# A decoder layer with a retrieved-expert mixer: the fifth densely expanded token tile goes back to gathers

## Chip, cores and metric

The kernel runs on one core of a Trainium2 chip. The metric is the device time of one execution in microseconds (us). Times inside the program come from one profiled execution and count from its first instruction.

## What is computed

One decoder layer over 1024 tokens of width 1024, in float32. A token mixer (gated convolution beside dilated window attention) gives the stream `h`; behind it stands a mixer of retrieved experts (PEER), where the change lies. For each token and each of 8 heads, two sets of 128 keys are scored, the 16 best of each set are paired, and the 16 best pairs are kept: 128 of 16384 experts per token, each with a gate. The expert weights are the rows of two tables, `down` and `up`, of 16384 x 1024 each.

```python
q = (xf @ w_query).reshape(T, PEER_HEADS, 2, PEER_D_HALF)
s = jnp.einsum('thcd,hckd->thck', q, sub_keys)
top_s, top_i = lax.top_k(s, PEER_TOPK)
...
best_s, pos = lax.top_k(cand_s, PEER_TOPK)
idx = jnp.take_along_axis(cand_i, pos, axis=-1)          # T x 8 x 16 expert numbers
gates = jax.nn.softmax(best_s, axis=-1)
...
a = jax.nn.gelu(jnp.einsum('cd,ced->ce', xc, expert_down[ic]))
return jnp.einsum('ce,ced->cd', gc * a, expert_up[ic])    # sum of 128 up rows per token
```

The result is added to the stream, and a last RMS norm scales it.

## The kernel before

The tokens are cut into eight tiles of 128 (128 tokens lie on the 128 partitions). Tiles 0 to 3 are the first half, tiles 4 to 7 the second. The mixer runs for the first half, then for the second; the retrieved experts of the two halves are computed in two different ways, at the same time.

**The side stream (first half, `experts()`).** For each tile and each of 128 experts per token, an indirect DMA on GpSimd's queue gathers one row of `down` per token (128 rows of 4 KB, L851) into one of ROWS = 4 buffers `row`, and VectorE forms its dot product with the token's vector `ut` (L853). After 128 such steps a GELU and the gates give `a`. Then 128 rows of `up` per token are gathered into the same buffers (`rowu`, L867), and VectorE adds each, scaled by its `a`, to `acc` (L869). A norm and a store end the tile. One gather with its VectorE operation is called a step here.

**The dense part (second half, `dense()`).** For all 16384 experts the hidden activations of the 512 tokens are computed by TensorE: `hidden(q)` takes four blocks of 128 experts, loads their `down_t` weights (`raw`, split by L165 and L167 into a high and a low part, so that three matmuls give float32 accuracy), and leaves `ga`. The first STORED = 27 groups go to memory (`a_d`) and are fetched again; four more are held, and the last one is computed late. Meanwhile a routing table is built: `choose` finds experts and gates of a tile, `build` turns them by one-hot matrices (`oa`, `ob`, L940 to L948) and small matmuls (`psg`, L953) into a table of gates per expert and token, which goes to memory as `g_d`. In the up phase, for each of 32 groups, `weigh(q)` multiplies `ga` by the table (`gg`), splits it (`hh`, `hl`), and TensorE multiplies it with the split up rows (`uh`, `ul`, L181 and L182) into PSUM tiles: `held` stays over all groups, `psu` is added to `rest` in SBUF after each (L1067). At the end the sums meet the stream in `h1b` (L1071), and each tile is normed and stored.

**The fifth tile.** `XT = (1,)` makes tile 1 of the first half a mixture: its `down` rows are gathered as above, but after the GELU its gated activations go to `given`, which builds a routing table of them; in the up phase `weigh` reads it as `gx`, splits it (`xh`, `xl`, L978 and L979) and TensorE multiplies it with the same up rows as a fifth tile. So the side stream has 512 down steps and 384 up steps, and the up phase five tiles.

**What sets the order.** The main program yields shares of its work, divided by PACE_B, PACE_C or PACE_D, and the side stream advances by as many steps as have come due. A scheduler then fixes one list per engine. Each engine works its own list through from top to bottom.

Of the kernel before, what the change touches and what calls it, by code (L numbers as in the profile page):

```python
# [8 lines left out]
F32 = mybir.dt.float32  # L9
F32R = mybir.dt.float32r  # L10
I32 = mybir.dt.int32
U32 = mybir.dt.uint32
AF = mybir.ActivationFunctionType
ALU = mybir.AluOpType
# [3 lines left out]
P = 128  # L18
T = 1024
TH = 512  # L20
# [10 lines left out]
ROWS = 4  # L31
TC = 32
NB = 4
PACE_B = 2.0
PACE_D = 2.0
PACE_C = 2.2
RATE_G = 0.8
STORED = 27
HOLD = 4
RAWS = 4  # L40
HILO = 2
# [4 lines left out]
AT_P = 6  # L46
CHOOSE = (0, 1, 2, 3)
ORDER = (0, 1, 2, 3)
TILES = (4, 5, 6, 7, 1)
STB = 2  # L50
XT = (1,)
GXB = 2
XHB = 1
UPS = 7
NW = 2
NS = 2
# [9 lines left out]
def hybrid_layer(ctx, tc, x, xT, pos, rotc, norm_mix, w_proj, w_v, conv_w, w_conv_out, w_attn_out,  # L66
                 gate_bias, w_out, norm_ffn, w_query, sub_keys, down, down_t, up, final_norm, out):
    nc = tc.nc
    V, S, G, PE = nc.vector, nc.scalar, nc.gpsimd, nc.tensor
# [6 lines left out]
    ex = ctx.enter_context(tc.tile_pool(name="ex", bufs=1))  # L76
# [73 lines left out]
    y_d = dram.tile([2, KD, P, TH], F32, name="y_d")  # L150
    s_d = dram.tile([3, P, 16, P], F32, name="s_d")
    a_d = dram.tile([STORED, P, NB, TH], F32, name="a_d")
    g_d = dram.tile([(TH + len(XT) * P) // TC, P, P, TC], F32, name="g_d")


    def row_scale(src):
# [677 lines left out]
            queue.dma_start(out[r, c], acc[:, c])  # L834


    xready = {}

    def experts():
        for tt in ORDER:  # L840
            r = slice(tt * P, tt * P + P)
            if tt:
                for _ in later[tt]:
                    pass
            idx, gate = picked[tt]
            ut = ex.tile([P, D], F32, tag="ut", name="ut")
            SIDE.dma_start(ut, u2_d[r])
            a = ex.tile([P, P], F32, tag="a", name="a")
            for e in range(P):
                row = gt.tile([P, D], F32, tag="row", name="row")  # L850
                G.indirect_dma_start(out=row, out_offset=None, in_=down,  # L851
                                     in_offset=bass.IndirectOffsetOnAxis(ap=idx[:, e:e + 1], axis=0))
                V.tensor_tensor_reduce(out=row, in0=row, in1=ut, scale=1.0, scalar=0.0, op0=ALU.mult,  # L853
                                       op1=ALU.add, accum_out=a[:, e:e + 1])
                yield 1.0
            S.activation(a, a, AF.Gelu)
            if tt in XT:
                ax = ex.tile([P, P], F32, tag=f"ax{tt}", name="ax")
                V.tensor_tensor(ax, a, gate, op=ALU.mult)
                xready[tt] = (idx, ax)  # L860
                continue
            V.tensor_tensor(a, a, gate, op=ALU.mult)
            acc = ex.tile([P, D], F32, tag="acc", name="acc")
            SIDE.dma_start(acc, h1_d[r])  # L864
            for e in range(P):
                row = gt.tile([P, D], F32, tag="row", name="rowu")
                G.indirect_dma_start(out=row, out_offset=None, in_=up,  # L867
                                     in_offset=bass.IndirectOffsetOnAxis(ap=idx[:, e:e + 1], axis=0))
                V.scalar_tensor_tensor(acc, row, a[:, e:e + 1], acc, op0=ALU.mult, op1=ALU.add)  # L869
                yield 1.0  # L870
            st = ex.tile([P, 3], F32, tag="st", name="st")
            nfin = gt.tile([P, D], F32, tag="row", name="nfin")
            SIDE.dma_start(nfin, final_norm.to_broadcast([P, D]))
            S.activation(ut, acc, AF.Square, accum_out=st[:, 0:1])
            finish(acc, r, st, nfin, SIDE)


    def dense():
# [2 lines left out]
        bld = ExitStack()  # L881
        den = bld.enter_context(tc.tile_pool(name="den", bufs=2))
        NG = P // NB
        NT = 4 + len(XT)
        gas = {}

        def hidden(q):
# [18 lines left out]
            yield from choose(lambda hc: s_t[tt][:, hc], True, got)  # L906
            yield from build(got[0], tt * P // TC)

        def given(k):
            while XT[k] not in xready:  # L910
                next(result["side"])
            idx, ax = xready[XT[k]]
            part = den.tile([P, 2, P], U32, tag="part", bufs=1, name="part")
            V.tensor_scalar(part[:, 0], idx.bitcast(U32), 7, None, op0=ALU.logical_shift_right)
            V.tensor_scalar(part[:, 1], idx.bitcast(U32), 127, None, op0=ALU.bitwise_and)
            name = den.tile([P, 2, P], F32, tag="name", bufs=1, name="name")
            V.tensor_copy(name, part)
            yield from build((name[:, 0], name[:, 1], ax), (TH + k * P) // TC)

        def routes():  # L920
            for k in range(len(XT)):
                yield from given(k)
            for tt in range(4):
                yield from chosen(tt)

        def build(srcs, c0):
                sT = den.tile([P, 3, P], F32, tag="sT", bufs=STB, name="sT")
                for j, src in enumerate(srcs):
                    ps = psc.tile([P, P], F32, tag="sc", name="ps_t")
                    PE.transpose(ps, src, ident)  # L930
                    S.copy(sT[:, j], ps)
                for c in range(c0, c0 + P // TC):
                    stg = [den.tile([P, 32, TC], F32, tag="stg", bufs=STG, name="stg") for _ in range(4)]
                    for t4 in range(TC // 4):
                        ps = psc.tile([P, 4, P], F32, tag="sc", name="psg")
                        k0 = (c * TC + t4 * 4) % P
                        i1, i2, gv = (sT[:, j, k0:k0 + 4] for j in range(3))
                        oa = den.tile([P, 4, P], F32, tag="oa", bufs=OBUF, name="oa")
                        ob = den.tile([P, 4, P], F32, tag="ob", bufs=OBUF, name="ob")
                        V.tensor_tensor(oa, iota[:, None, :].to_broadcast([P, 4, P]),  # L940
                                        i1[:, :, None].to_broadcast([P, 4, P]), op=ALU.is_equal)
                        if t4 % 2 == 0:
                            for t in range(4):
                                S.activation(ob[:, t], iota, AF.Abs, bias=i2[:, t:t + 1], scale=-1.0)
                            S.activation(ob, ob, AF.Relu, bias=ones[:, 0:1], scale=-1.0)
                            V.tensor_tensor(ob, ob, gv[:, :, None].to_broadcast([P, 4, P]), op=ALU.mult)
                        else:
                            V.tensor_tensor(ob, iota[:, None, :].to_broadcast([P, 4, P]),  # L948
                                            i2[:, :, None].to_broadcast([P, 4, P]), op=ALU.is_equal)
                            for t in range(4):  # L950
                                S.mul(ob[:, t], ob[:, t], gv[:, t:t + 1])
                        for t in range(4):
                            PE.matmul(ps[:, t], ob[:, t], oa[:, t], start=True, stop=True)  # L953
                        for w in range(4):
                            S.copy(stg[w][:, :, t4 * 4:t4 * 4 + 4],
                                   ps[:, :, 32 * w:32 * w + 32].rearrange("p t i -> p i t"))
                        yield 1.1
                    for w in range(4):
                        nc.sync.dma_start(g_d[c, :, 32 * w:32 * w + 32], stg[w])

        def weigh(q):
            gg = m8.tile([P, TH // TC, NB, TC], F32, tag="big", name="gg")
            nc.sync.dma_start(gg, g_d[:TH // TC, :, NB * q:NB * q + NB].rearrange("c j i t -> j c i t"))
            ga = gas.pop(q)
            hh, hl = bigr("hh"), bigr("hl")
            for ii in range(NB):
                v = ga[:, ii].rearrange("p (c t) -> p c t", t=TC)
                V.tensor_tensor(v, v, gg[:, :, ii], op=ALU.mult)
                split(hh[:, ii], hl[:, ii], ga[:, ii])
            parts = [(hh[:, :, tt * P:tt * P + P], hl[:, :, tt * P:tt * P + P]) for tt in range(4)]  # L970
            for k in range(len(XT)):
                gx = up_p.tile([P, P // TC, NB, TC], F32, tag="gx", bufs=GXB, name="gx")
                c0 = (TH + k * P) // TC
                nc.sync.dma_start(gx, g_d[c0:c0 + P // TC, :, NB * q:NB * q + NB].rearrange("c j i t -> j c i t"))
                xh = up_p.tile([P, NB, P], F32R, tag="xh", bufs=XHB, name="xh")
                xl = up_p.tile([P, NB, P], F32R, tag="xl", bufs=XHB, name="xl")
                view = [t.rearrange("p i (c t) -> p c i t", t=TC) for t in (xh, xl)]
                S.copy(view[0], gx)  # L978
                V.tensor_tensor(view[1], gx, view[0].bitcast(F32), op=ALU.subtract)  # L979
                parts.append((xh, xl))  # L980
            return parts

        ready = {}
# [96 lines left out]
    begin()  # L1080
    for _ in mixer(0):
        pass
    side = result["side"] = experts()
    due = 0.0

    def main():
# [67 lines left out]
```

## Time and profile before

| | us |
|---|---|
| median of 3 runs | 3464.77 |
| lowest and highest run | 3463.74, 3466.05 |
| the profiled execution | 3463.79 |
| its span, first to last instruction | 3462.0 |

| engine | busy, us | share of the span |
|---|---|---|
| TensorE (PE) | 3316.7 | 96% |
| VectorE (DVE) | 2766.8 | 80% |
| ScalarE (ACT) | 1486.4 | 43% |
| GpSimd (POOL) | 1193.4 | 34% |

Read the shares with care: they are means over stages that have different limits. PE's busy time counts matmuls, PEld the weight loads beside them. POOL is busy while it writes a DMA's descriptors, not while the data move.

### The profile page before, as it was taken

What the parts mean: (1) busy time and instruction counts of PE and PEld (TensorE: products, weight loads), DVE (VectorE), ACT (ScalarE), POOL (GpSimd) and SP (SyncE); (2) the same over time, 40 slices, a digit from 0 to 9 for tenths busy, and PEclk for the clock granted to TensorE, in tenths of its full rate; (3) what the DMA queues carried; (4) which work ended last, traced back from release to release, by engine and by line L of the source; (5) the groups of instructions that cost most, each with busy time, mean ns of one, the idle gap of its engine ahead of it and who ended that gap; (6) DMA issues with size and microseconds to landing.
All of it is one profiled execution on the core that took longest, in us unless ns stands there. A gap on an engine that the chain in (4) does not pass through costs nothing.

```text
span 3462.0 us, 47124 instructions
## 1 busy us (share of the span) xinstructions
PE 3316.7 (96%) x15923; PEld 2702.5 (78%) x15923; DVE 2766.8 (80%) x5646; ACT 1486.4 (43%) x3371; POOL 1193.4 (34%) x944
## 2 busy tenths in 40 slices
PE   7999999999979999989899999999999999999998
PEld 6787877888767877667777878888887788887787
DVE  4333345689998888988999999998887888888887
ACT  3444445443333445333325776887632222222222
POOL 0000000004554235555444334354444334444443
PEclk9999999999979999999999999999999999999999
DMA  4232335669987678898898989989898999989996
GB/s 129 78 110 89 122 107 180 246 210 323 308 281 256 227 246 298 305 340 309 301 329 300 342 288 343 349 313 366 334 323 311 331 326 332 337 324 329 332 348 230
DMA packets 364307, 948.08 MB, mean 274 GB/s; under 512 B 33952, under 2 KB 127648, under 8 KB 356640
## 3 DMA queue, kind: packets, MB, share of 16 engines
q1 hardware_dynamic: 232016, 465.27, 38.8%
q0 software_dynamic: 132048, 479.78, 38.4%
q8 instruction: 126, 2.06, 0.2%
q14 instruction: 117, 0.96, 0.1%
HBM read 843.15 MB, written 95.49 MB: 271 GB/s over the span
## 4 chain that ended last, share of the span: by engine, by line
PE 28%; issue 16%; DVE 14%; DMA 14%; POOL 8%; ACT 2%; POOLq 0%; DVEq 0%; SPq 0%; ACTq 0%
DMA rowu<-in_up,idx 6%; PE ps L178 6%; PE ps L176 6%; PE ps L177 6%; POOL row L851 4%; DVE row L853 4%; DMA row<-in_down,idx 4%; POOL rowu L867 3%; PE psg L953 2%; DVE lo L167 2%; DVE acc L869 1%; DMA g_d<-stg 1%; DMA gg<-g_d 1%; PE held L177 1%; PE held L178 1%
## 5 line engine op out<-in xcount | busy, mean ns | idle before, releaser
L851 POOL DMA_INDIRECT row<-in_down,idx x512 | 641.5, 1253 | 896.6 <-DVE a L853 504.3
L867 POOL DMA_INDIRECT rowu<-in_up,idx x384 | 528.4, 1376 | 622.5 <-DVE acc L869 496.6
L165 ACT CAST hi<-raw 128x1024 fp32r<-128x1024 f32 x368 | 388.0, 1054 | 713.5 <-PE ps L177 506.8
L853 DVE CUSTOM_DVE_ANT_0 row<-row,ut 128x1024 f32<-128x1024 f32 x512 | 618.8, 1214 | 62.8 <-DMA row<-in_down,idx 60.8
L167 DVE TENSOR_TENSOR lo<-raw,hi 128x1024 fp32r<-128x1024 f32 x368 | 448.4, 1219 | 264.6 <-ACT hi L165 252.6
L178 PE MATMUL ps<-vhi,lo 128*128 128x512 f32 (+1 forms) x1408 | 536.7, 382 | 22.0 <-DVE lo L167 21.7
L869 DVE SCALAR_TENSOR_TENSOR acc<-rowu,a,acc 128x1024 f32<-128x1024 f32 x384 | 491.2, 1279 | 66.4 <-DMA rowu<-in_up,idx 64.3
L176 PE MATMUL ps<-vhi,hi 128*128 128x512 f32 (+1 forms) x1408 | 531.8, 378 | 12.3 <-ACT hi L165 7.6
L177 PE MATMUL ps<-vlo,hi 128*128 128x512 f32 (+1 forms) x1408 | 530.6, 377 | 0.0
L176 PE MATMUL ps<-uhi,hi 128*128 128x512 f32 x1024 | 408.3, 400 | 6.1 <-ACT hi L165 3.6
L178 PE MATMUL ps<-uhi,lo 128*128 128x512 f32 x1024 | 408.5, 399 | 2.5 <-DVE lo L167 2.3
L177 PE MATMUL ps<-ulo,hi 128*128 128x512 f32 x1024 | 408.3, 399 | 0.5 <-DVE ulo L182 0.5
L178 PEld LDWEIGHTS ps<-vhi,lo 128*128 128x128 f32 x1408 | 269.7, 192 | 75.7 <-DVE lo L167 31.9
L176 PEld LDWEIGHTS ps<-vhi,hi 128*128 128x128 f32 x1408 | 270.4, 192 | 61.3 <-ACT hi L165 12.4
L177 PEld LDWEIGHTS ps<-vlo,hi 128*128 128x128 f32 x1408 | 269.7, 192 | 45.0
L177 PE MATMUL held<-ul,hh 128*128 128x512 f32 x624 | 246.5, 395 | 10.0 <-DVE ul L182 10.0
L178 PE MATMUL held<-uh,hl 128*128 128x512 f32 x624 | 244.1, 391 | 0.0
L176 PEld LDWEIGHTS ps<-uhi,hi 128*128 128x128 f32 x1024 | 193.8, 189 | 52.7 <-ACT hi L165 5.5
L178 PEld LDWEIGHTS ps<-uhi,lo 128*128 128x128 f32 x1024 | 193.6, 189 | 47.4 <-DVE lo L167 5.8
L176 PE MATMUL held<-uh,hh 128*128 128x512 f32 x624 | 230.5, 393 | 0.0
L177 PEld LDWEIGHTS ps<-ulo,hi 128*128 128x128 f32 x1024 | 193.6, 189 | 42.8 <-DVE ulo L182 1.7
L864 POOL DMA_DIRECT2D acc<-h_d x3 | 1.8, 615 | 640.9 <-DMA h_d<-h 640.9
(350 smaller groups left out, 6133.8 us busy)
## 6 DMA issues: line engine op xcount, KB each, us to landing
raw<-in_w_proj SPq DMA_DIRECT2D x128, 512.0 KB
raw<-in_down_t SPq DMA_DIRECT2D x128, 512.0 KB
rawu<-in_up SPq DMA_DIRECT2D x128, 512.0 KB
g_d<-stg SPq DMA_DIRECT2D x80, 512.0 KB
gg<-g_d SPq DMA_DIRECT2D x32, 1024.0 KB
a_d<-ga SPq DMA_DIRECT2D x27, 1024.0 KB
ga<-a_d SPq DMA_DIRECT2D x27, 1024.0 KB
raw<-in_w_query SPq DMA_DIRECT2D x48, 512.0 KB
```

The costliest lines, as they stand in the source:

```text
L165: S.copy(hi, raw)
L167: V.tensor_tensor(lo, raw, hi.bitcast(F32), op=ALU.subtract)
L176: PE.matmul(ps, l[0], r[0], start=first, stop=False)
L177: PE.matmul(ps, l[0], r[1], start=False, stop=False)
L178: PE.matmul(ps, l[1], r[0], start=False, stop=last)
L851: G.indirect_dma_start(out=row, out_offset=None, in_=down, in_offset=bass.IndirectOffsetOnAxis(ap=idx[:, e:e + 1], axis=0))
L853: V.tensor_tensor_reduce(out=row, in0=row, in1=ut, scale=1.0, scalar=0.0, op0=ALU.mult, op1=ALU.add, accum_out=a[:, e:e + 1])
L864: SIDE.dma_start(acc, h1_d[r])
L867: G.indirect_dma_start(out=row, out_offset=None, in_=up, in_offset=bass.IndirectOffsetOnAxis(ap=idx[:, e:e + 1], axis=0))
L869: V.scalar_tensor_tensor(acc, row, a[:, e:e + 1], acc, op0=ALU.mult, op1=ALU.add)
L953: PE.matmul(ps[:, t], ob[:, t], oa[:, t], start=True, stop=True)
```

## The change

Tile 1 is no longer in the dense part: `XT` and all that hangs on it is removed (`given`, the fifth part of `weigh`, the larger `g_d`), so its up rows are gathered and summed as for tiles 0, 2 and 3. With it come other paces and a smaller STORED.

```diff
-PACE_B = 2.0
-PACE_D = 2.0
-PACE_C = 2.2
+PACE_B = 1.8
+PACE_D = 1.8
+PACE_C = 2.0
-STORED = 27
+STORED = 24
-TILES = (4, 5, 6, 7, 1)
+TILES = (4, 5, 6, 7)
-XT = (1,)
-GXB = 2
-XHB = 1
...
             S.activation(a, a, AF.Gelu)
-            if tt in XT:
-                ax = ex.tile([P, P], F32, tag=f"ax{tt}", name="ax")
-                V.tensor_tensor(ax, a, gate, op=ALU.mult)
-                xready[tt] = (idx, ax)
-                continue
             V.tensor_tensor(a, a, gate, op=ALU.mult)
...
-        NT = 4 + len(XT)
+        NT = 4
...
-        def given(k):
-            while XT[k] not in xready:
-                next(result["side"])
...
-            yield from build((name[:, 0], name[:, 1], ax), (TH + k * P) // TC)
...
         def routes():
-            for k in range(len(XT)):
-                yield from given(k)
             for tt in range(4):
                 yield from chosen(tt)
...
-            for k in range(len(XT)):
-                gx = up_p.tile([P, P // TC, NB, TC], F32, tag="gx", bufs=GXB, name="gx")
...
-                S.copy(view[0], gx)
-                V.tensor_tensor(view[1], gx, view[0].bitcast(F32), op=ALU.subtract)
-                parts.append((xh, xl))
             return parts
```

Lines move up by 3 to 33 with it: in the new kernel the down gather is L846, its dot product L848, the up gather L857 and its sum L859, the addition of `held` to `h1b` L1038.

The list of POOL, where tile 1 passes from down rows to what follows. Before:

```order
L864 DMA acc<-h_d 128x1024
L851 DMA row<-in_down,idx 128x1024 x125
L847 DMA ut<-u_d 128x1024
L851 DMA row<-in_down,idx 128x1024 x125
L867 DMA rowu<-in_up,idx 128x1024 x128
```

The same place in the new list:

```order
L854 DMA acc<-h_d 128x1024
L846 DMA row<-in_down,idx 128x1024 x122
L857 DMA rowu<-in_up,idx 128x1024 x128
L863 DMA nfin<-in_final_norm 128x1024
L846 DMA row<-in_down,idx 128x1024 x3
L842 DMA ut<-u_d 128x1024
L831 DMA out<-acc 128x1024
```

Before, the down rows of tile 1 are followed at once by those of tile 2; now 128 gathers of up rows stand between them, with the norm and the store of the tile.

The list of VectorE, near its end, where the side stream's last sums and the first additions of `held` into `h1b` meet. Before:

```order
L869 SCALAR_TENSOR_TENSOR acc<-rowu,a,acc 128x1024 x2
L979 TENSOR_TENSOR xl<-gx,xh 128x4x4x32
L869 SCALAR_TENSOR_TENSOR acc<-rowu,a,acc 128x1024 x3
L1071 TENSOR_TENSOR h1b_28941<-h1b_28941,held_22681 128x512
L1071 TENSOR_TENSOR h1b_28941<-h1b_28941,psu 128x512
L200 TENSOR_SCALAR st<-st 128x1
L1071 TENSOR_TENSOR h1b_28942<-h1b_28942,psu 128x512
```

The last addition of `held` in the new list (ISA with `row` is a down dot product, ISA `a` the reading of its sum):

```order
L1042 TENSOR_TENSOR sts<-sts 128x1
L848 ISA row,a<-row,ut 128x1024
L848 ISA a 128x1
L1042 TENSOR_TENSOR sts<-sts 128x1
L1038 TENSOR_TENSOR h1b_27664<-h1b_27664,held_21632 128x512
L199 RECIPROCAL sts<-sts 128x1
L848 ISA row,a<-row,ut 128x1024
```

And the end of VectorE's new list:

```order
L848 ISA row,a<-row,ut 128x1024
L848 ISA a 128x1
L852 TENSOR_TENSOR a<-a,ge 128x128
L859 SCALAR_TENSOR_TENSOR acc<-rowu,a,acc 128x1024 x128
L197 TENSOR_SCALAR st<-st 128x1
L199 RECIPROCAL st<-st 128x1
L200 TENSOR_TENSOR st<-st 128x1
L201 TENSOR_TENSOR st<-st 128x1
L202 TENSOR_SCALAR st<-st 128x1
L203 TENSOR_TENSOR st<-st 128x1
L830 SCALAR_TENSOR_TENSOR acc<-acc,st,nfin 128x1024
```

Before, all 896 steps stand ahead of the first addition of `held`. In the new list 796 of 1024 stand ahead of the last one, and 100 dot products and 128 up sums behind it. Counted in the same way, 314 steps stand ahead of the 240th operation of L167 before and 312 now (L164 there), and 598 ahead of the first split of up rows (`ul`) before and 538 now.

## Rows read from the trace of the kernel before

**Rows 1.** The page: busy us (share of the span) and instructions; DMA in all.

```profile
PE 3316.7 (96%) x15923; PEld 2702.5 (78%) x15923; DVE 2766.8 (80%) x5646; ACT 1486.4 (43%) x3371; POOL 1193.4 (34%) x944
...
DMA packets 364307, 948.08 MB, mean 274 GB/s; under 512 B 33952, under 2 KB 127648, under 8 KB 356640
```

**Rows 2.** The stage cuts: VectorE by time, and the instructions of tile `ul`.

```profile
1639.93 1.22 DVE L167 TENSOR_TENSOR lo<-raw,hi 128x1024 fp32r<-128x1024 f32 x1
...
L182 DVE TENSOR_TENSOR ul<-rawu,uh x126: 1209/1216/1239, 2514.2 to 3421.6; 128x1024 fp32r<-128x1024 f32 x126
```

**Rows 3.** Busy time by stage: stretch, its length, then the engines.

```profile
core 0: us, PE busy (x) PEld busy (x) DVE busy (x) ACT busy (x) POOL busy (x), PEclk, DMA share, GB/s
0.00:1640.00 1640.00, 1554.28 (x7659) 1248.02 (x7660) 1164.91 (x2791) 689.41 (x1384) 427.10 (x358) 0.98 0.64 219
1640.00:2514.00 874.00, 839.77 (x4272) 703.69 (x4271) 817.73 (x1816) 556.95 (x1650) 370.71 (x286) 0.99 0.89 327
2514.00:3452.60 938.60, 922.59 (x3995) 750.75 (x3993) 778.08 (x1024) 239.12 (x334) 395.60 (x301) 1.00 0.90 322
...
2514.00:3400.00 886.00, 869.99 (x3767) 707.92 (x3766) 734.63 (x951) 224.87 (x303) 378.97 (x288) 1.00 0.92 330
```

**Rows 4.** The end, by time: start us, us, engine, line, operation, [idle before].

```profile
3426.12 1.86 POOL L867 DMA_INDIRECT rowu<-in_up,idx  x1 [0.65 <-DVE acc L869]
...
3431.34 1.28 DVE L869 SCALAR_TENSOR_TENSOR acc<-rowu,a,acc 128x1024 f32<-128x1024 f32 x1 [1.05 <-DMA rowu<-in_up,idx]
...
3438.52 0.57 POOL L834 DMA_DIRECT2D out<-acc  x1 [9.96 <-DVE acc L833]
...
3452.23 0.39 PE L178 MATMUL held<-uh_end,xl 128*128 128x512 f32 x1
```

**Rows 5.** Groups by line: count, busy us, mean ns, then idle before.

```profile
L867 POOL DMA_INDIRECT rowu<-in_up,idx x384 | 528.4, 1376 | 622.5 <-DVE acc L869 496.6 <-DMA rowu<-in_up,idx 32.0 <-issue 18.8
L869 DVE SCALAR_TENSOR_TENSOR acc<-rowu,a,acc 128x1024 f32<-128x1024 f32 x384 | 491.2, 1279 | 66.4 <-DMA rowu<-in_up,idx 64.3
L167 DVE TENSOR_TENSOR lo<-raw,hi 128x1024 fp32r<-128x1024 f32 x368 | 448.4, 1219 | 264.6 <-ACT hi L165 252.6 <-DMA qp<-rraw 4.9 <-DMA raw<-in_w_proj 4.8
L940 DVE TENSOR_TENSOR oa<-iota,sT 128x512 f32<-128x512 f32 x160 | 105.6, 681 | 7.1 <-PE psg L953 6.2 <-ACT sT L931 0.6 <-issue 0.2
L1067 DVE TENSOR_TENSOR rest<-rest,psu 128x512 f32<-128x512 f32 x120 | 80.2, 679 | 2.3 <-PE psu L178 2.3
L948 DVE TENSOR_TENSOR ob<-iota,sT 128x512 f32<-128x512 f32 x80 | 54.1, 680 | 0.0
L979 DVE TENSOR_TENSOR xl<-gx,xh 128x512 fp32r<-128x512 f32 x32 | 21.8, 680 | 0.0
```

**Rows 6.** One stretch, tile `ps` (weight matmuls), then `psg` (table): PE first.

```profile
2200.00:2500.00 300.00, 241.89 (x1016) 186.98 (x1015) 25.89 (x42) 1.00 0.91 338
...
2200.00:2500.00 300.00, 74.53 (x608) 74.09 (x608) 60.12 (x304) 1.00 0.91 338
```

**Rows 7.** DMA queues from 2514 to 3452.6 us: packets, MB, share.

```profile
q1 hardware_dynamic: 121569, 141.85, 45.5%
q0 software_dynamic: 43776, 159.40, 44.0%
```

**Rows 8.** A sum on VectorE, and the gather that it releases on POOL.

```profile
3381.41 1.28 DVE L869 SCALAR_TENSOR_TENSOR acc<-rowu,a,acc 128x1024 f32<-128x1024 f32 x1 [0.44 <-DMA rowu<-in_up,idx]
...
3382.97 0.94 POOL L867 DMA_INDIRECT rowu<-in_up,idx  x1 [1.39 <-DVE acc L869]
```

**Rows 9.** The densest gathers, POOL by time: first and last of 28.

```profile
943.83 0.94 POOL L851 DMA_INDIRECT row<-in_down,idx  x1 [1.13 <-DVE a L853]
...
998.69 1.58 POOL L851 DMA_INDIRECT row<-in_down,idx  x1 [0.94 <-DVE a L853]
```

**Rows 10.** Instructions of tile `rowu`: ns min/median/max, first and last start.

```profile
L869 DVE SCALAR_TENSOR_TENSOR acc<-rowu,a,acc x384: 1233/1278/1344, 1119.2 to 3431.3; 128x1024 f32<-128x1024 f32 x192
```

More of the change, by code (lines that the diff above doesn't have):

```diff
@@ L152, in hybrid_layer @@
     a_d = dram.tile([STORED, P, NB, TH], F32, name="a_d")
-    g_d = dram.tile([(TH + len(XT) * P) // TC, P, P, TC], F32, name="g_d")
+    g_d = dram.tile([TH // TC, P, P, TC], F32, name="g_d")
     def row_scale(src):
@@ L834, in finish @@
             queue.dma_start(out[r, c], acc[:, c])
-    xready = {}
     def experts():
@@ L907, in chosen @@
             yield from build(got[0], tt * P // TC)
-        def given(k):
-            while XT[k] not in xready:
-                next(result["side"])
[L912 to L917, printed above, removed]
-            yield from build((name[:, 0], name[:, 1], ax), (TH + k * P) // TC)
         def routes():
-            for k in range(len(XT)):
-                yield from given(k)
             for tt in range(4):
@@ L970, in weigh @@
             parts = [(hh[:, :, tt * P:tt * P + P], hl[:, :, tt * P:tt * P + P]) for tt in range(4)]
-            for k in range(len(XT)):
-                gx = up_p.tile([P, P // TC, NB, TC], F32, tag="gx", bufs=GXB, name="gx")
[L973 to L977, printed above, removed]
-                S.copy(view[0], gx)
-                V.tensor_tensor(view[1], gx, view[0].bitcast(F32), op=ALU.subtract)
-                parts.append((xh, xl))
             return parts
@@ L1082, in hybrid_layer @@
         pass
-    side = result["side"] = experts()
+    side = experts()
     due = 0.0
```

## The prediction

> **What bounds the kernel now.** I began with the busy table of the page [rows 1]: TensorE is busy 96% of the span, VectorE 80%, and the DMA engines move 948 MB. A share of the span hides stages with different limits, so I cut the span at two places that can be found in both programs. The first is the 240th weight split of L167, at about 1640 us, when the hidden activations of the dense half begin; the second is the first split of up rows, at 2514 us [rows 2]. The busy times of the stages [rows 3] show TensorE with 840 of 874 us in the middle stage and 923 of 939 us in the last; VectorE has 818 of 874 us in the middle one, so there the two are nearly level, and in the last one VectorE has 17% to spare. Between 2514 and 3400 us a matmul record takes 886/3767 = 0.235 us of wall time. So before the change every matmul taken out of the last two stages is worth close to its time, as long as the program ends with TensorE. It does: the last gather sum starts at 3431.3 us, the last matmul ends at 3452.6 us, and the span ends at 3462.0 us [rows 4]. The stream of gathers is finished 20 us before the dense work; that is the fact to watch.
>
> **What goes.** The fifth tile costs 32 x 2 x 4 x 3 = 768 matmuls of 512 columns in the last stage. Its routing table costs 128 matmuls of the program, 256 records in the trace, in the middle stage, and on VectorE 64 operations of 0.68 us (32 `oa`, 32 `ob`), then 32 splits `xl` of 0.68 us and 60 of the 120 additions into `rest`, also 0.68 us [rows 5]. On the queues go 16 of the 80 writes `g_d<-stg` and the 32 reads `gx<-g_d` of 256 KB.
>
> **What comes.** 128 gathers of 0.5 MB on POOL, and 128 sums of 1.28 us on VectorE [rows 5]; without the dense tile 1024 gather steps have to be done instead of 896. STORED falls from 27 to 24, which moves 12 weight matrices (288 matmuls, 12 splits of 1.22 us) from the middle stage to the last and drops three 1 MB writes and reads.
>
> **What moves, which decides.** VectorE runs its list in order. In the list of before 314 gather steps stand ahead of the first cut, 598 ahead of the second, and all 896 ahead of the first addition of `held`. In the new list it is 312, 538, and at the last addition of `held` (which needs TensorE's last matmul) 796. Behind that addition stand 100 down dot products and 128 up sums, with no dense work left. The paces were lowered from 2.0 and 2.2 to 1.8 and 2.0, which asks for more steps per unit of dense work, but the list itself says that they don't fit: 228 steps come after the dense work. The new kernel has two ends, one behind the other.
>
> **Stage by stage, on the profiled execution's own time.**
> First stage: the lists differ by two gather steps, I leave it at 1640 us.
> Middle stage, 874 us. TensorE loses 288 matmuls at 241.89/1016 = 0.238 us and 256 table records at 74.53/608 = 0.123 us [rows 6], 68.6 + 31.4 = 100 us: 774 us if its idle time stays. VectorE loses 58 steps at 1.28 us, 64 operations of 0.68 us and 12 splits of 1.22 us: 74 + 44 + 15 = 132 us, so 818 - 132 = 686 us; at the share of before, 818/874 = 0.936, that is 733 us. VectorE was the tighter one in the first half of this stage, TensorE in the second; I take 750 us, nearer to VectorE's, and keep 733 to 774.
> Last stage up to the last matmul, 938.6 us. Matmul records go from 3995 to 3995 - 768 + 288 = 3515; at 0.235 us that is 826 us, and at TensorE's busy time alone (922.59/3995 = 0.231) 812 us. The cover is the DMA: its share is 0.90 of 938.6 us, 845 us [rows 3]. 40 fewer gathers are 21 MB at the software queue's price (44.0% of 938.6 us for 159.4 MB, 2.59 us per MB), 54 us; `gx` and three `ga` reads are 11.5 MB at the hardware queue's (45.5% for 141.85 MB, 3.01 us per MB), 35 us; 6.3 MB of weights come to 19 us [rows 7]. 845 - 70 = 775 us; at the share of 0.92 that the stretch 2514 to 3400 us holds [rows 3], 842 us. I take 830 us and keep 812 to 842. VectorE needs 778 - 51 - 22 - 41 + 15 = 679 us there, which fits.
> So the last addition of `held` comes at 1640 + 750 + 830 = 3220 us, 232 us earlier than now. That is the gain.
>
> **The tail.** Before the change no stretch has gathers alone, so I bound a step from both sides. Four row buffers are in use, so four steps share one loop: gather, landing, VectorE's operation, and back to the gather. The last gather starts at 3426.12 us and its sum, which waited for it, at 3431.34 us: 5.22 us, with 1.86 us on POOL [rows 4]. From the end of a sum to the start of the next gather I read 3382.97 - (3381.41 + 1.28) = 0.28 us [rows 8]. The loop is 5.22 + 1.28 + 0.28 = 6.78 us, a step 1.70 us. With the 0.94 us that POOL takes when VectorE stands still [rows 8], the loop is 5.86 us and a step 1.46 us. From the other side: the densest stretch of gathers, from 943.83 to 998.69 us, has 27 steps of 2.03 us [rows 9], with VectorE doing other work between them. I take 1.75 us, because it is a little above the blocked loop, and gathers so close also queue behind each other; ends 1.46 and 2.03. The tail is 228 x 1.75 = 399 us (333 to 463). Behind the last sum the chain stays as now: the sum started at 3431.34 us, the store of `acc` was issued from 3438.52 to 3439.09 us [rows 4], and I add 2 us for its landing: 10 us, 11 with the end of the program.
> Sum: 3220 + 399 + 11 = 3630 us of span, and 1.8 us around it (3463.79 against 3462.0) make 3632 us. The profiled execution lies 1 us below the median of the runs, which I leave aside.
>
> **Why POOL's time in the loop varies.** A gather that started at 3426.12 us while a sum was running took 1.86 us, others 0.94 us [rows 4, 8]; that is the difference between my 1.70 and 1.46. The Trainium skill (SBUF — State Buffer, section "SBUF: two separate sides") says that VectorE and GpSimd share a port pair as an exclusive lock, so that a POOL-issued DMA cannot write its descriptors while VectorE holds it; the trace agrees with 1.86 against 0.94 us.
>
> **Rivals.**
> One: in the tail POOL and VectorE exclude each other at every step. A step is then 1.28 + 0.94 = 2.22 us and the tail 506 us: 1640 + 750 + 830 + 506 + 11 + 2 = 3739 us. For it: 1.86 us is 0.94 and most of a sum. Against it: none of 384 sums took over 1.344 us [rows 10], so VectorE does not wait for POOL. The lock of that page of the Trainium skill, taken strictly, is this case.
> Two: with the dense transfers gone, landings get so short that the tail runs at VectorE's pace, 1.28 us: 292 us, 3525 us in all. Against it: even the unblocked loop gives 1.46 us with four buffers.
> Three, not slower: everything that I count as waiting is queueing behind gathered rows and dense transfers, and goes with them. TensorE then has its busy time alone, 1554 + 740 + 812 = 3106 us [rows 3], and the tail VectorE's: 3106 + 292 + 11 + 2 = 3411 us, faster by 1.5%. It decides from 168 us on beyond my sum, or a step under 1.02 us if the dense work keeps my time; no operation of a step is so short. For it: TensorE is idle 145 us in all. Against it: the first stage, where most of that lies, is unchanged.
> That the change does not do what it says can be excluded by the lists: POOL has 512 up gathers and SP no `gx`.
>
> **How the numbers follow.** The forecast, 3632 us, has 0.78, rival one 0.08, rival two 0.11, rival three 0.03. The ends of the terms add up to 1640 + 733 + 812 + 333 + 13 = 3531 and 1640 + 774 + 842 + 463 + 13 = 3732 us; terms rarely lie at the same end together, so the forecast's own spread is 3545 to 3710 us. For 8 in 10 I reach down to rival two and a little up: 3520 to 3715 us; outside are rivals one and three and some of the forecast. A change of 0.2% is about what a measurement of this kernel can tell from none. Faster by more has rival three alone, 0.03; no change gets 0.01, for the space between rivals two and three; slower 0.96.
>
> **What would show it.** After the change TensorE must be idle for some 400 us at the end, with POOL's L846 and L857 and VectorE's L848 and L859 alone at work; the last matmul should end near 3220 us, and the gather steps behind it number 228. In the tail VectorE waits for DMA at nearly every step and POOL for VectorE. The middle stage should take about 750 us, the last about 830 us. I am wrong if the last matmul comes after 3290 us (then the dense stages were bound by DMA or VectorE after all), if a tail step is under 1.4 or over 2.1 us, or if TensorE works to the end.

## The result and the profile after

The changed kernel takes 3696.03 us (median of 4 runs, 3689.86 to 3699.20), the kernel before 3465.41 us: a ratio of 1.0652, 95% interval 1.0628 to 1.0677. The forecast was 3632 us. The profiled execution took 3689.86 us, with a span of 3688.0 us.

The page's busy table and its 40 slices show it at once. TensorE loses 1027 matmul records and 209 us against [rows 1], and is idle in the last five slices; there the granted clock stands at 0.5, the lower of its two levels (1.2 GHz), and TensorE has no more work.

```profile
PE 3108.1 (84%) x14896; PEld 2531.4 (69%) x14896; DVE 2838.6 (77%) x5609; ACT 1407.7 (38%) x3062; POOL 1401.9 (38%) x1075
...
PE   7999999999899999898999999999899999900000
...
PEclk9999999999799999899999999999999999955555
DMA  4233345778886788988887899998889999888886
```

The same cuts as in [rows 3], and a fourth stretch from the last matmul on (busy us of each engine, granted clock, DMA share, GB/s):

```profile
0.00:1637.50 1637.50, 1558.12 (x7659) 1248.41 (x7660) 1162.04 (x2787) 690.21 (x1384) 409.64 (x356) 0.98 0.65 219
1637.50:2401.20 763.70, 734.78 (x3711) 618.45 (x3710) 699.41 (x1584) 471.35 (x1352) 351.69 (x231) 0.99 0.86 312
2401.20:3230.60 829.40, 815.16 (x3530) 664.50 (x3528) 675.20 (x862) 239.13 (x310) 359.85 (x260) 0.99 0.92 329
3230.60:3688.00 457.40, 0.00 (x0) 0.00 (x0) 301.98 (x381) 6.99 (x16) 280.74 (x230) 0.50 0.80 270
```

The dense work ends 222 us earlier than before (3230.6 against 3452.6 us), and behind it come 457 us in which nothing is full: VectorE is busy 302 us, POOL 281 us, the DMA engines 0.80. That is the picture of a loop that waits for itself: gather, landing, VectorE's operation, and back to the gather into the same buffer. The two places where the engines pass to the tail are the last matmul, and the last addition of `held`, behind which 228 steps follow:

```profile
3230.17 0.39 PE L175 MATMUL held<-uh_end,hl 128*128 128x512 f32 x1
...
3235.92 0.68 DVE L1038 TENSOR_TENSOR h1b<-h1b,held 128x512 f32<-128x512 f32 x1
```

Inside the tail's up part, the instructions of tile `rowu` (ns min/median/max, first and last start) give the step: 220.6 us over 116 intervals, 1.90 us. Over all 228 steps, from the addition at 3235.9 us to the end of the last sum at 3672.3 us, it is 1.91 us.

```profile
L859 DVE SCALAR_TENSOR_TENSOR acc<-rowu,a,acc x117: 1283/1285/1350, 3439.3 to 3659.9; 128x1024 f32<-128x1024 f32 x117
L857 POOL DMA_INDIRECT rowu<-in_up,idx x116: 932/938/1997, 3440.0 to 3658.4; - x116
```

By time, gathers on POOL and sums on VectorE (start us, us, what they waited for):

```profile
3544.81 0.94 POOL L857 DMA_INDIRECT rowu<-in_up,idx  x1 [0.59 <-DVE acc L859]
3547.53 1.89 POOL L857 DMA_INDIRECT rowu<-in_up,idx  x1 [1.79 <-DVE acc L859]
3549.72 1.90 POOL L857 DMA_INDIRECT rowu<-in_up,idx  x1 [0.30 <-DMA rowu<-in_up,idx]
3551.93 1.02 POOL L857 DMA_INDIRECT rowu<-in_up,idx  x1 [0.30 <-issue]
3553.25 1.70 POOL L857 DMA_INDIRECT rowu<-in_up,idx  x1 [0.30 <-issue]
...
3545.98 2.63 DVE L859 SCALAR_TENSOR_TENSOR acc<-rowu,a,acc 128x1024 f32<-128x1024 f32 x2 [1.44 <-DMA rowu<-in_up,idx]
3549.53 2.60 DVE L859 SCALAR_TENSOR_TENSOR acc<-rowu,a,acc 128x1024 f32<-128x1024 f32 x2 [0.92 <-DMA rowu<-in_up,idx]
3552.86 1.28 DVE L859 SCALAR_TENSOR_TENSOR acc<-rowu,a,acc 128x1024 f32<-128x1024 f32 x1 [0.73 <-DMA rowu<-in_up,idx]
3555.85 1.28 DVE L859 SCALAR_TENSOR_TENSOR acc<-rowu,a,acc 128x1024 f32<-128x1024 f32 x1 [1.71 <-DMA rowu<-in_up,idx]
```

The gather of 3544.81 us serves the second sum of the pair at 3549.53 us, which starts near 3550.85 us, 6.0 us later; that sum ends at 3552.13 us and frees its buffer, but the next gather into it starts only at 3553.25 us, 1.1 us later, because POOL was still at the gather of 3551.93 us. In these rows VectorE waits for a landing before every sum or pair of sums. Over 116 such steps, from the records of the trace: 5.64 us from a gather's start to its sum's start (about 5.2 until its last row is written, about 0.4 behind that), 1.29 us for the sum, 0.66 us to the next gather; 7.6 us for four buffers.

The end, two sums in one row and the store behind them:

```profile
3669.72 2.61 DVE L859 SCALAR_TENSOR_TENSOR acc<-rowu,a,acc 128x1024 f32<-128x1024 f32 x2 [0.57 <-DMA rowu<-in_up,idx]
...
3677.60 0.56 POOL L831 DMA_DIRECT2D out<-acc  x1 [9.08 <-DVE acc L830]
```

### The profile page after: what moved, and what is told of

Its sections match the earlier page's. It is cut to its first block, busy times and chain, and to the rows that moved or that the text cites. A ratio compares the mean times of both kernels' runs of the same rounds, so it can differ in the third digit from the quotient of the medians.

```text
span 3688.0 us, 44975 instructions
## 1 busy us (share of the span) xinstructions
PE 3108.1 (84%) x14896; PEld 2531.4 (69%) x14896; DVE 2838.6 (77%) x5609; ACT 1407.7 (38%) x3062; POOL 1401.9 (38%) x1075
## 4 chain that ended last, share of the span: by engine, by line
PE 35%; issue 13%; DVE 12%; DMA 12%; POOL 9%; ACT 2%; POOLq 0%; SPq 0%; DVEq 0%; ACTq 0%
POOL row L846 6%; PE ps L175 5%; PE ps L173 5%; PE ps L174 5%; DMA rowu<-in_up,idx 5%; DMA row<-in_down,idx 4%; DVE row L848 3%; POOL rowu L857 3%; PE held L175 3%; PE held L174 3%; PE held L173 3%; DVE lo L164 2%; PE psg L930 2%; DVE acc L859 1%; PE psu L175 1%
## 5 line engine op out<-in xcount | busy, mean ns | idle before, releaser
L857 POOL DMA_INDIRECT rowu<-in_up,idx x512 | 740.2, 1446 | 818.1 <-DVE acc L859 606.5
L846 POOL DMA_INDIRECT row<-in_down,idx x512 | 636.4, 1243 | 729.3 <-DVE a L848 394.9
L859 DVE SCALAR_TENSOR_TENSOR acc<-rowu,a,acc 128x1024 f32<-128x1024 f32 x512 | 655.4, 1280 | 112.3 <-DMA rowu<-in_up,idx 109.5
L848 DVE CUSTOM_DVE_ANT_0 row<-row,ut 128x1024 f32<-128x1024 f32 x512 | 619.8, 1217 | 138.9 <-DMA row<-in_down,idx 135.6
L164 DVE TENSOR_TENSOR lo<-raw,hi 128x1024 fp32r<-128x1024 f32 x368 | 448.6, 1220 | 271.7 <-ACT hi L162 267.3
L174 PE MATMUL held<-ul,hh 128*128 128x512 f32 x752 | 295.0, 392 | 2.0 <-DVE ul L179 2.0
L175 PE MATMUL held<-uh,hl 128*128 128x512 f32 x752 | 296.1, 394 | 0.0
L173 PE MATMUL held<-uh,hh 128*128 128x512 f32 x752 | 292.6, 390 | 0.0
L178 ACT CAST uh<-rawu 128x1024 fp32r<-128x1024 f32 x126 | 132.2, 1050 | 374.7 <-PE held L175 123.7
```

The costliest lines, as they stand in the source:

```text
L164: V.tensor_tensor(lo, raw, hi.bitcast(F32), op=ALU.subtract)
L173: PE.matmul(ps, l[0], r[0], start=first, stop=False)
L174: PE.matmul(ps, l[0], r[1], start=False, stop=False)
L175: PE.matmul(ps, l[1], r[0], start=False, stop=last)
L178: S.copy(hi, src)
L846: G.indirect_dma_start(out=row, out_offset=None, in_=down, in_offset=bass.IndirectOffsetOnAxis(ap=idx[:, e:e + 1], axis=0))
```

## The experiments

Theory: the change frees TensorE, but the list leaves 228 steps behind the dense work, and each costs a quarter of that loop. Rivals: the steps were badly placed and the dense stages have room for them; the paces or STORED made the kernel slow; something other than the loop sets the step. Ratios are to the kernel before, run on the same chip.

**All steps forced ahead of the end of the dense work.**

```diff
-                    split(uh, ul, raw)
+                    S.copy(uh, raw)
+                    with tc.issue_after(steps[-1].ins):
+                        V.tensor_tensor(ul, raw, uh.bitcast(F32), op=ALU.subtract)
```

Here `steps` holds the VectorE operation of every step that the program has yielded so far.

> The changed kernel, but the split of up rows (ul, L179) is ordered behind the gather steps that the program yielded ahead of it, so that all 1024 steps stand ahead of the last addition of held and none behind it (228 behind it in the changed kernel). Theory: the gathered rows are too many bytes for the dense stages; the DMA queues are busy 657 us of the middle stage and 763 us of the last one in the changed kernel, 228 gathers at 1.39 us add 317 us, and at a share of 0.89 to 0.92 both stages together take 1890 to 1950 us: about 3580 us (3550 to 3615), faster than the changed kernel, still slower than before. Rival 1: the dense stages have room for the steps and only the list was bad: about 3260 us. Rival 2: a step costs its 1.91 us wherever it stands: about 3690 us.

Measured: 3816.8 us, ratio 1.0985 (1.0956 to 1.1014), slower than the changed kernel and than theory and both rivals said. The tail is gone, but the two dense stages took 1016 and 1155 us instead of 764 and 829 us. The middle stage, cut in three, and the up phase:

```profile
1634.90:2400.00 765.10, 736.55 (x3713) 618.72 (x3712) 699.01 (x1586) 470.61 (x1353) 359.39 (x231) 0.99 0.87 312
2400.00:2500.00 100.00, 17.54 (x77) 13.94 (x75) 68.37 (x111) 8.45 (x14) 60.43 (x49) 0.61 0.85 286
2500.00:2651.30 151.30, 2.08 (x4) 1.16 (x4) 99.86 (x136) 3.14 (x4) 94.08 (x80) 0.50 0.84 278
2651.30:3806.00 1154.70, 889.36 (x3448) 698.32 (x3448) 803.96 (x977) 228.34 (x305) 489.62 (x361) 0.87 0.80 280
```

Up to 2400 us the middle stage runs as in the changed kernel. Then TensorE all but stops for 251 us, and the other 128 of the stage's 354 steps go through with hardly any dense work beside them, at 1.9 to 2.1 us each: the forced order did not spread them, it put a second tail into the middle of the program. The first split of up rows now stands behind 666 steps instead of 538, and in ScalarE's list the GELU of a tile (`a`), which needs all dot products of the tile, comes before the next copies to `uh` (us in total, times, longest us):

```profile
ACT a L853 <- DVE a L850: 172.7, 1, 172.7
PE held L173 <- ACT uh L1016: 186.6, 1, 186.6
PE held L174 <- DVE ul L1018: 46.4, 1, 46.4
```

In the up phase TensorE waits for VectorE's `ul`, which stands behind gather steps in the list:

```profile
PE held L174 <- DVE ul L1018: 216.0, 44, 46.4
PE held L173 <- ACT uh L1016: 70.5, 16, 13.6
```

The DMA share is 0.80 there, so the bytes were not the limit, and my expectation fell with that. A step's interval in this up phase is 2.9 us, a quarter of a loop of 11.7 us, of which about 6.7 us go by until the rows are written under the load of the dense transfers and about 3.1 us until VectorE's list comes to them. TensorE's own work takes longer too: the granted clock is 0.87 instead of 0.99, and 3448 matmul records are busy for 889 us, where 3530 were for 815 us in the changed kernel. In all the 228 forced steps add 578 us to the two stages, 2.5 us each; the tail that they replace was 457 us. Against this list, the tail that the scheduler left is the cheaper place. Whether steps spread finely over the middle stage, with four buffers, would fit, no run shows.

**Three more buffers from the up phase on.**

```diff
+    def buffer(name):
+        turns[0] += 1
+        k = turns[0] % (ROWS + EXTRA)          # EXTRA = 3
+        pool = more[0] if more and k < EXTRA else gt
+        return pool.tile([P, D], F32, tag="row", name=name)
...
-                row = gt.tile([P, D], F32, tag="row", name="rowu")
+                row = buffer("rowu")
```

> The changed kernel with three more row buffers (7 instead of 4) from the up phase on; 218 steps stand behind the last addition of held instead of 228. Theory: the 1.91 us of a step in the tail is a quarter of one loop of 7.6 us through four buffers; with seven the loop would allow 1.09 us, and the next limit is the DMA engines, busy 0.82 of the tail, so 1.55 to 1.6 us per step: tail 218 x 1.6 = 349 us, about 3600 us in all. Rival 1: loop alone, then VectorE's 1.29 us per step: 281 us, about 3535 us. Rival 2: POOL and VectorE hinder each other and the buffers don't matter: 1.9 us per step, about 3680 us.

Measured: 3551.06 us, ratio 1.0233 (1.0204 to 1.0262), 145 us less than the changed kernel, with the last matmul at 3229.5 us as there. The tail's step is 1.37 us (165.4 us over 121 intervals):

```profile
L867 POOL DMA_INDIRECT rowu<-in_up,idx x127: 933/1017/1758, 3346.5 to 3518.8; - x127
L869 DVE SCALAR_TENSOR_TENSOR acc<-rowu,a,acc x122: 1283/1285/1330, 3353.6 to 3519.0; 128x1024 f32<-128x1024 f32 x122
```

Busy time in that tail, engines as in the stages above:

```profile
3240.00:3520.00 280.00, 0.00 (x0) 0.00 (x0) 263.80 (x309) 0.31 (x1) 216.11 (x206) 0.50 1.00 392
```

The loop through four buffers was the limit, which rules out rival 2. The floor below it is lower than I said: rival 1, VectorE's own 1.29 us, is nearly reached, with VectorE busy 264 of 280 us. The DMA share is 1.00 at 392 GB/s, which is 1.34 us for the 0.524 MB of a gather, so the DMA engines are as near to their end; this run does not separate the two. My 1.55 us came from the share of 0.82 in a tail that was not full; a share at part load does not scale to a time at full load.

**Narrow sums.** In the last tile the sums take 64 of 1024 columns.

```diff
-                V.scalar_tensor_tensor(acc, row, a[:, e:e + 1], acc, op0=ALU.mult, op1=ALU.add)
+                w = slice(0, 64 if tt == 3 else D)
+                V.scalar_tensor_tensor(acc[:, w], row[:, w], a[:, e:e + 1], acc[:, w], op0=ALU.mult, op1=ALU.add)
```

> The changed kernel; in the last tile of the side stream (tile 3) the 128 up sums on VectorE take 64 of the 1024 columns, the other columns are left out; the gathers are whole. Theory: VectorE's 1.28 us leaves the loop and POOL is no longer held up by it (1.22 us in the mean falls to 0.94): the loop falls from 7.63 us to about 5.9 to 6.1 us, 1.5 us per up step, with the DMA engines at 1.55 us right beside: 1.55 us per step, the up part of the tail falls from 242 to about 198 us, about 3645 us in all. Rival 1: VectorE bounds the step: it falls by 1.16 us to 0.75 us, about 3545 us. Rival 2: landing bounds it: 1.9 us, no change.

Measured: 3661.48 us in one run. The up step is 1.63 us (200.2 us over 123 intervals); POOL's gather takes 0.94 us throughout:

```profile
L860 DVE SCALAR_TENSOR_TENSOR acc<-rowu,a,acc x124: 283/284/286, 3439.7 to 3639.9; 128x64 f32<-128x64 f32 x124
L857 POOL DMA_INDIRECT rowu<-in_up,idx x122: 932/936/941, 3440.4 to 3638.0; - x122
```

VectorE gave up 1.00 us per step and the step fell by 0.27 us, a quarter of it, as a loop over four buffers wants; neither rival fits. POOL's 1.22 us in the mean had come from VectorE's wide sums, since its maximum falls from 1.997 to 0.941 us when they are narrow. But the 0.28 us that POOL gained did not come out of the loop: from a gather's start to its sum's start are 5.78 us here and 5.6 to 5.7 us in the changed kernel, by the records of both traces. My 1.55 us had counted on it.

**The removal alone.** Tile 1's up rows are left out: no dense tile, no gathers.

```diff
-            for e in range(P):
+            for e in range(0 if tt == 1 else P):
                 row = gt.tile([P, D], F32, tag="row", name="rowu")
```

> The changed kernel with the up rows of tile 1 left out altogether: no dense tile and no gathers for it, 896 steps as before, 62 of them behind the last addition of held. This is the removal alone. Theory: the dense work again ends near 3240 to 3250 us, and 62 steps at 1.91 us and the end of 16 us follow: about 3385 us. So the removal alone is worth about 80 us and the 128 gathers put back cost about 305 us. Rival 1: the side stream fits once it has 896 steps: about 3260 us. Rival 2: every step left out is worth its 1.91 us and no more: 3690 - 245 = 3445 us.

Measured: 3422.76 us, ratio 0.9856 (0.9829 to 0.9884), between theory and rival 2. The dense work ended at 3280.8 us, not near 3245 us: 834 steps instead of 796 stand ahead of its end, and the middle stage, with 266 gather steps instead of 226, took 809 us. The 62 steps behind it cost 138 us with the end:

```profile
1633.80:2442.50 808.70, 748.37 (x3707) 626.18 (x3706) 743.79 (x1728) 472.11 (x1353) 334.87 (x271) 0.97 0.89 320
2442.50:3280.80 838.30, 819.53 (x3537) 666.09 (x3535) 675.45 (x870) 243.67 (x318) 348.36 (x259) 0.99 0.92 325
3280.80:3418.70 137.90, 0.00 (x0) 0.00 (x0) 90.02 (x100) 2.53 (x8) 74.33 (x63) 0.51 0.77 259
```

So without any step put back the removal is worth 1.4%, 50 us (3472.6 for the kernel before in the same set of runs, less 3422.8), and not the 80 us that I expected, because the side stream is then what ends last. By the two ratios (1.0652 - 0.9856) the 128 gathers put back cost 276 us, 2.2 us each.

**Forced, with seven buffers; then spread by other paces.** The edit of the first experiment on top of the second; in the other kernel besides PACE_B = 2.3, PACE_C = 2.6, PACE_D = 1.5, and the last store on SP's queue.

> All 1024 steps forced ahead of the last addition of held as in e1_forced, with seven row buffers instead of four from the up phase on. Theory, formed after e1_forced: its up phase took 1155 us because a step's loop through four buffers is 11.7 us long under the load of the dense transfers (6.7 us to the landing, 3.1 us until VectorE's list reaches it), and TensorE stood 216 us waiting for ul behind such steps. With seven buffers the rows wait for VectorE instead, and the up phase is bound by its bytes, 273 + 100 gathers more x 0.524 = 325 MB at about 340 GB/s, 960 us; the middle stage still has four buffers and stays at 1016 us: 1635 + 1016 + 960 + 10 = about 3620 us. Rival: the order itself is at fault (ul behind the steps stops TensorE whatever the buffers): about 3810 us, as e1_forced.

> As e5_forced7, with paces 2.3, 2.6 and 1.5, so that 520 steps instead of 666 stand ahead of the up phase and 497 inside it, 7 behind the last addition of held; the last tile is stored through SP's queue. Theory: middle stage as in the changed kernel or a little shorter (2370 to 2400 us), up phase 273 + 239 x 0.524 = 398 MB at 340 to 360 GB/s, 1105 to 1170 us: 3485 to 3580 us, about 3520 us; not below before, because 128 up rows by gather are 67 MB for which the DMA queues have no room, while TensorE has. Rival: with the steps spread and buffers enough the removed matmuls come out as a gain: 3420 us or less.

Measured: 3674.47 us, ratio 1.059 (1.0565 to 1.0615), and 3598.42 us, ratio 1.0368 (1.0347 to 1.039). The up phases, forced first:

```profile
2658.90:3667.00 1008.10, 857.85 (x3448) 681.33 (x3448) 801.93 (x979) 230.35 (x305) 499.30 (x359) 0.92 0.87 320
2397.20:3581.00 1183.80, 915.06 (x3515) 713.45 (x3513) 969.50 (x1228) 235.41 (x312) 700.35 (x504) 0.87 0.92 338
```

The forced up phase falls from 1155 to 1008 us, which is 147 of the 195 us above the 960 us that I gave for its bytes; its middle stage, still with four buffers, has the same stop and takes 1022 us. In the spread kernel that stop is gone, and the middle stage takes 750 us. Its up phase takes 1184 us, a little above the 1105 to 1170 us that I gave: 239 gathers more than in the changed kernel for 354 us more, 1.5 us each. That is no less than the 1.37 us of a step in the tail with seven buffers, and the rival, 3420 us or less, is out for this list. TensorE still waits, most for VectorE's list, 168.5 us in the spread kernel:

```profile
PE held L175 <- DVE ul L1029: 168.5, 43, 9.7
PE held L174 <- ACT uh L1027: 77.8, 22, 7.9
```

Neither reaches the 3551 us of the list that the scheduler made itself. How much of the rest is this coarse order, how much the bytes and how much the lower clock (0.92 and 0.87 in these up phases, 1.00 in that of the scheduler's list) stays open.

**Paces and STORED.** The changed kernel with those of before; the kernel before with the new ones; and with STORED = 24 alone.

> The changed kernel with the paces and STORED of before (2.0, 2.0, 2.2 and 27): 236 steps behind the last addition of held instead of 228. Theory: the list is set by the scheduler's own picture of the gathers and hardly by the paces; 8 steps more at 1.91 us, about 3705 us (3680 to 3720). Rival: the new paces or the smaller STORED made the kernel slow: 3465 us or less.

> The kernel before with the new paces and STORED = 24 alone; the fifth dense tile stays, and no step stands behind the last addition of held. Theory: within 0.5% of before, 3450 to 3482 us. Rival: the paces or STORED cost time by themselves: over 3550 us.

> The kernel before with STORED = 24 alone (paces 2.0, 2.0, 2.2, fifth dense tile kept). Theory, formed after e8_new_paces_alone was 74 us slower than before: the 12 weight matrices that go from the middle stage to the up phase cost TensorE 288 x 0.235 = 68 us there, and the middle stage gives little back for them because VectorE bounds it: about 3535 us (3520 to 3545). Rival: the paces made e8 slow: within 0.5% of before.

Measured: 3702.61 us, ratio 1.0679 (1.0661 to 1.0697), no difference from the changed kernel that the intervals resolve; 3538.78 us, ratio 1.0216 (1.0187 to 1.0245), against my theory and short of the rival's 3550 us; and 3546.11 us, ratio 1.0233 (1.0209 to 1.0257). So in the kernel before the paces do nothing that the runs resolve and STORED = 24 costs 2.3%; in the changed kernel the two, put back together, do nothing. The stages of the last of the three, beside [rows 3]:

```profile
1647.00:2504.60 857.60, 794.10 (x4041) 666.33 (x4040) 798.50 (x1802) 541.00 (x1630) 371.22 (x282) 0.97 0.89 321
2504.60:3536.80 1032.20, 984.70 (x4224) 797.76 (x4224) 798.84 (x1038) 256.17 (x354) 392.70 (x305) 0.98 0.84 296
```

The up phase grows by 94 us: 68 us for the 288 matmuls at 0.235 us, and 22 us for a single wait of TensorE:

```profile
PE held L176 <- ACT xh L978: 22.1, 1, 22.1
```

The middle stage gives back only 16 us, though TensorE's busy time there falls by 46 us; VectorE's falls by 19 us, so I read the stage as bound by VectorE's list, which no run of its own shows. In the changed kernel, which has no table of a fifth tile to build, the middle stage took 764 us with STORED = 24 and 828 us with 27, nearly the 288 matmuls:

```profile
1641.50:2469.40 827.90, 801.13 (x3999) 673.47 (x3998) 743.45 (x1646) 488.89 (x1376) 395.01 (x256) 0.99 0.88 315
```

There the stage follows TensorE, busy 96 to 97% of it, as long as the list holds 226 or 251 gather steps in it; with 266 steps and the matmuls of STORED = 24, in the kernel without tile 1's up rows, it took 809 us.

**One more stored group** in the kernel before, to turn this round.

```diff
-STORED = 27
+STORED = 28
```

> The kernel before with STORED = 28 instead of 27, so that the last four weight matrices also go into the middle stage. Theory, the other way round: the up phase loses 96 matmuls, 22 us, the middle stage grows by 5 to 20 us: 3445 to 3465 us, about 3455 us, 0.3% faster than before. Rival: TensorE's 22 us only move: within 0.2%.

Measured: 3460.61 us, ratio 0.9992 (0.9977 to 1.0007): no difference. No version that I ran with the whole computation beats the kernel before.

**The last store on SP's queue.**

```diff
-            finish(acc, r, st, nfin, SIDE)
+            finish(acc, r, st, nfin, nc.sync if tt == ORDER[-1] else SIDE)
```

> The changed kernel with the store of the side stream's last tile issued from SP's queue instead of POOL's. Theory: of the 17 us from the start of the last up sum to the end of the span about 7 us are POOL's drain, which ends at 3687.4 us though the store's last data were written at 3680.2 us; with SP's queue the span ends some 3 us after the data, 5 to 7 us earlier, about 3689 us against 3696. Rival: the end is bound by the store itself: no difference.

Measured: 3686.69 us, ratio 1.0636 (1.0612 to 1.0661), which overlaps the changed kernel's. The traces, for SP's queue that of the slowest of its four runs, show the 7 us all the same: from the start of the last sum, in each kernel the last of its kind, to the end of the span are 10.0 us (3688.11 to 3698.1) instead of 17.0 us (3671.04 to 3688.0). With POOL's queue the store's last data are written at 3680.2 us, and a DRAIN instruction of POOL runs on from 3677.6 to 3687.2 us, just before the end of the program. Last sum and store with SP's queue:

```profile
3688.11 1.29 DVE L859 SCALAR_TENSOR_TENSOR acc<-rowu,a,acc 128x1024 f32<-128x1024 f32 x1 [0.89 <-DMA rowu<-in_up,idx]
...
3694.40 0.33 SPq L831 DMA_DIRECT2D out<-acc  x1
```

## Why the prediction was right, and where its sizes were off

The mechanism held: 228 steps stand behind the dense work in VectorE's list, the kernel has two ends one behind the other, and the second is a loop through four buffers. By its terms:

- First stage: 1640 us said, 1637.5 us measured.
- Middle stage: 750 us said, 763.7 us measured, between the two limits and nearer to TensorE's 774 us. The pair with STORED = 27 and 24 speaks for TensorE once the table work is gone; I had leaned to VectorE.
- Last stage to the last matmul: 830 us said, 829.4 us measured. The DMA share is the 0.92 that I took, but TensorE's 0.235 us for each of 3530 matmul records gives the time by itself. The last addition of `held` came 5.3 us after the matmul, behind gather steps; I had counted nothing for that.
- Tail: 399 us said, 436 us measured. This is the term that was mis-sized: 1.75 us a step against 1.91. I read 5.22 us from gather to sum off a single gather of [rows 4]; the mean in the tail is 5.64 us. I took 0.28 us from sum to gather from [rows 8]; the mean is 0.66 us, since a gather often finds POOL still at the one before. The densest stretch of [rows 9], 2.03 us, was the nearer bound.
- End: 11 us said, 15.7 us measured from the end of the last sum. In [rows 4] the side stream's store is not the last thing, so POOL's DRAIN (3438.5 to 3446.1 us there) was covered by the dense work; here it is the end.

The misses, -2.5 + 13.7 - 0.6 + 5.3 + 37.4 + 4.7, are the 58 us between 3630 and 3688.0 us of span; the median lies another 6 us above the profiled execution. No miss of size was made up by another: nearly all lie on the slow side.

Rival one (POOL and VectorE exclude each other, 2.22 us a step) is out: 1.91 us with four buffers, 1.37 us with seven. The hindrance goes one way: gathers took up to 2.0 us in the tail, sums never over 1.35 us, as [rows 10] had said. And my lower bound of 1.46 us took POOL's 0.94 us for a gain of the whole loop, which the narrow sums did not show; besides, the gather of [rows 8] did not find VectorE standing still throughout, since the next sum started at 3383.34 us, before that gather ended. Rival two (VectorE's pace) is out with four buffers and nearly true with seven. Rival three fell with them: the first stage kept its idle time, and the removal alone gave 50 us. Where I argued that no operation of a step is as short as 1.02 us, I overlooked POOL's gather of 0.94 us; VectorE's 1.28 us is what excludes it.

What I did not see is that the paces and STORED do nothing to the changed kernel, and how little a list forced by hand mends. With four buffers it stopped TensorE in the middle of the program. With seven, and the steps spread by other paces, each gather that was moved into the up phase cost 1.5 us there. In the expectation of the first experiment I gave the bytes as the limit of the dense stages; there they were not, in the spread kernel the time came near to it.

## What to carry to other kernels

When work moves from the engine that ends last to a stream that runs beside it, count in the built lists how much of that stream stands behind the last dense instruction: that part is paid in full, whatever the busy shares say. As long as none of its engines is full, a stream of gathers through n buffers costs its whole loop over n per step, and the loop has to be read as a mean where gathers are dense, with the queueing on the issuing engine in it. Before forcing such a stream earlier, add buffers: here three more gave back 145 us with the scheduler's own list, and no list forced by hand came down to that. And look in a forced list for the place where the dense engine now waits, on every engine's list that feeds it.

## What I had not expected of the hardware

- POOL's gathers took 0.94 us at the longest beside sums of 64 columns, and up to 2.0 us beside sums of 1.28 us, in the same place of the program; yet the rows came no sooner (5.78 us from gather to sum beside the narrow sums, 5.64 us beside the wide ones).
- A program that ends with a store from POOL's queue ended about 7 us later after its last sum than one whose store is on SP's queue (17.0 against 10.0 us).
- The DMA engines moved 392 GB/s of gathered 4 KB rows with no dense work beside them; mixed with the dense transfers no stage went above 346 GB/s before the change in a 100 us window, though shares of 0.93 to 0.95 looked full.
